# Retention's first weights in other places, five x tiles at the first MLP's end, x stores on ScalarE's queue, one raw ring for the first MLP weights, and token sums by DMA

## The chip, the core and the metric

One core of one Trainium2 chip runs the kernel. Its engines are TensorE (PE in the profile: matmuls and transposes), VectorE (DVE), ScalarE (ACT), GpSimd (POOL) and SyncE (SP, which here only issues DMAs). The metric is the device time of one execution in microseconds; the profile gives the span from the first to the last instruction and busy times within it.

## The reference, cut to what matters

A trunk of two layers over 512 latent tokens and 256 context tokens of width 1024, in float32. Layer 0 is neighbourhood attention beside gated chunks, layer 1 is retention with 8 heads; each is followed by a gated MLP with a convolution over three tokens. Only the latent tokens leave the second layer.

```python
h = modulate(rmsnorm(x, norm_g[i, 0]), sh1, sc1)          # and h_ctx alike
y = hybrid_na_sgu(...) if i % 2 == 0 else retention_mixer(...)
x = x + g1 * rmsnorm(y, norm_g[i, 1])
h = modulate(rmsnorm(x, norm_g[i, 2]), sh2, sc2)
x = x + g2 * rmsnorm(conv_ffn(h, ...), norm_g[i, 3])

def conv_ffn(h, w_in, conv_w, conv_b, w_out):             # D_FF = 2816, two halves
    a = dwconv3(h @ w_in, conv_w, conv_b)
    gate, up = jnp.split(a, 2, axis=-1)
    return (jax.nn.silu(gate) * up) @ w_out

# retention: q, k, v, g = split(h_lat @ w_in); kc, vc from h_ctx; per head a state from
# the context, a scan over chunks of 128 tokens in both directions, a norm, a gate, @ w_out
```

## The kernel before

**Precision.** A float32 matrix is used as a high part (ScalarE's copy, `split`, L68) and a low part (VectorE's difference, L69); a product is three matmuls, high by high, high by low, low by high (`mm3`, L93 to L96).

**Weights.** A block of 128 x 1024 weights (512 KB) is loaded by SyncE into a raw tile (a ring of three, `raw`) and split into a pair of tiles. Pairs `w0` to `w2` belong to a pool that lives through the whole program; further pairs (`w3` and up), and the MLP's extra raw tile `rawu`, belong to the pool of a phase (attention, first MLP, retention, second MLP). A phase's pool is closed before the next opens in the same memory.

**The end of a phase.** `out_last` multiplies the last features by the output weights, token tile by token tile (128 tokens each: 4 and 5 are context, 0 to 3 latent), and for each tile calls `residual` (L317 on): load the old x into `xt`; sums of squares of y on ScalarE (L291), y times the gate on VectorE (L323), a power on GpSimd (L296, L277), x = y * r + x on VectorE (L326), sums of squares again, the store of x to DRAM, then x scaled to unit size (L335, L336). The names of a profile row tell the token: `yb2r` is token tile 2 after attention, `xc3r` tile 3 after the first MLP, `xd` and `yd` after retention. TensorE then transposes the tile (`ht`, `htc`), ScalarE and VectorE modulate it (L364, L366, L412, L414), and the result is split.

**The entry of an MLP.** Columns and weights are taken as 2 x 2 blocks so that from the third block of features on seven block products do the work of eight; the needed sums of token blocks are made once (`block_sums`: `b11`, `b12`, `b21`, `b22` are the staged blocks `sa`, `sb`; L443 to L448), and split into `t1` to `t4` (`hs` holds `t2` and `t4`). The first two features (`plain`) are done without sums: products of `wp00`, `wp10`, `wp01` and `wp11` (gate or up, feature 0 or 1) with the first half of the tokens (`pf`), then with the second (`pf000b` and so on). In the first MLP `wp00`, `wp10` and `wp01` go to `w0`, `w1` and `w2`; in the second `wp00` to `w2`, the others to pairs of the phase's pool (`w5`, `w6`, `w4`).

**The entry of retention.** Head 0 projects k of the context (`rkc`), v of the context (`rn`, 48 matmuls), then k, q, v and the gate g of the latent tokens, half by half (`rk`, `rq`, `rn`). `rwk0`, `rwv00`, `rwv01`, `rwq0`, `rwg00` and `rwg01` are its weights, in `w0` to `w5` in this order.

**What sets the order.** The program is one long list of operations; the framework deals them out to the engines' queues by priority (place in the list) as they become ready in its own estimate, and adds the waits. So SyncE's loads need not stand in the order of the program. Each queue is then worked in order: what stands behind a waiting operation waits too. Layer-0 sums over features go to DRAM by adding DMAs on GpSimd's queue (L1468, L1470). Beside all this, the modulation of later layers (`ada_half`, L214) runs as background work.

Of the kernel before, what the change touches and what calls it, by code (L numbers as in the profile page):

```python
# [8 lines left out]
F32 = mybir.dt.float32  # L9
F32R = mybir.dt.float32r  # L10
# [3 lines left out]
ALU = mybir.AluOpType  # L14
AX = mybir.AxisListType

P = 128
D = 1024
# [22 lines left out]
class Trunk:  # L41
# [273 lines left out]
    def residual(self, t, y, gate, src, last, name, xt):  # L315

        V = self.V  # L317
        self.load(xt, src)
        hv = [slice(0, 512), slice(512, 1024)]
        for n, h in enumerate(hv):  # L320
            self.ssq(y[:, h], f"y{name}{t}", n)
        for h in hv:
            V.tensor_tensor(out=y[:, h], in0=y[:, h], in1=gate[:, h], op=ALU.mult)  # L323
        r = self.rms(f"y{name}{t}")
        for n, h in enumerate(hv):
            V.scalar_tensor_tensor(out=xt[:, h], in0=y[:, h], scalar=r, in1=xt[:, h], op0=ALU.mult, op1=ALU.add)  # L326
            if last:
                self.load(self.out[t * P : (t + 1) * P, h], xt[:, h])
            else:
                self.ssq(xt[:, h], f"x{name}{t}", n)  # L330
        if last:
            return
        self.load(self.xd[t], xt)
        r = self.rms(f"x{name}{t}")
        V.tensor_scalar(out=y[:, hv[0]], in0=xt[:, hv[0]], scalar1=r, scalar2=None, op0=ALU.mult)  # L335
        self.S.activation(y[:, hv[1]], xt[:, hv[1]], AF.Copy, scale=r)  # L336
# [59 lines left out]
    def build_piece(self, l, half, toks, c0, last, xn, ab):  # L396
        S, V = self.S, self.V
        w = P * len(toks)
        s = 1 if toks[0] > 3 else 0
        q = 512 // w  # L400
        for kk in range(KD // q):
            pt = self.ps(f"ht{l}{toks[0]}{kk}", "B", (P, q, w))
            for i in range(q):
                k = q * kk + i
                for j, t in enumerate(toks):
                    self.T.transpose(pt[:, i, j * P : (j + 1) * P], xn[t][:, k * P : (k + 1) * P], self.ident)
            for i in range(q):
                k = q * kk + i
                A, B = ab[:, s, 0, k : k + 1], ab[:, s, 1, k : k + 1]
                h = self.staged(l, half, k, 1)[:, 0, c0 : c0 + w]  # L410
                if i % 2 == 0:
                    S.activation(h, pt[:, i, :], AF.Identity, scale=A, bias=B)  # L412
                else:
                    V.tensor_scalar(out=h, in0=pt[:, i, :], scalar1=A, scalar2=B, op0=ALU.mult, op1=ALU.add)  # L414
        if not last:
            return
        if half:
            n = self.bn
            self.b12 = [
                [self.xp.tile([P, 2, n], F32R, name=f"b12{l}{x}{m}", tag=f"g{x}", bufs=4 if l else 3) for m in range(2)]  # L420
                for x in range(2)
            ]
        for m in range(4):
            src = self.staged(l, half, 2 * m, 2)
            if half and m < 2:
                self.split(self.b12[0][m], self.b12[1][m], src)
            else:
                b = self.blk[(11, 21)[m // 2] if not half else 22]
                ks = slice(2 * (m % 2), 2 * (m % 2) + 2)
                self.split(b[:, 0, ks, :], b[:, 1, ks, :], src)  # L430

    def block_sums(self, l):

        V, n = self.V, self.bn
        put = lambda b, m, src: self.split(b[:, 0, 2 * m : 2 * m + 2, :], b[:, 1, 2 * m : 2 * m + 2, :], src)
        for m in range(2):
            b11, b21 = (self.staged(l, 0, k + 2 * m, 2) for k in (0, 4))
            b12, b22 = (self.staged(l, 1, k + 2 * m, 2) for k in (0, 4))
            if l:
                t1 = self.t2k(f"t1{l}{m}", shape=(P, 2, n))  # L440
            else:
                t1 = self.bp.tile([P, 2, n], F32, name=f"t1{l}{m}", tag=f"y{1 + m}", bufs=1)
            V.tensor_tensor(out=t1, in0=b11, in1=b12, op=ALU.subtract)  # L443
            put(self.blk["t", 1], m, t1)
            V.tensor_tensor(out=b22, in0=b22, in1=b12, op=ALU.subtract)
            put(self.blk["t", 3], m, b22)
            V.scalar_tensor_tensor(out=b22, in0=b22, scalar=-1.0, in1=b11, op0=ALU.mult, op1=ALU.subtract)
            V.scalar_tensor_tensor(out=b12, in0=b22, scalar=-1.0, in1=b21, op0=ALU.mult, op1=ALU.subtract)  # L448
            yield
        hb = self.bp.tile([P, 6144], F32R, name=f"hs{l}", tag="h1", bufs=1)  # L450
        for i, x in enumerate((2, 4)):
            self.blk["t", x] = hb[:, 8 * n * i : 8 * n * (i + 1)].rearrange("p (x k c) -> p x k c", x=2, k=4)
        self.rest = hb[:, 16 * n :]
        for k, x in ((4, 2), (0, 4)):
            for m in range(2):
                put(self.blk["t", x], m, self.staged(l, 1, k + 2 * m, 2))
        yield
# [462 lines left out]
    def retention(self, y, final):  # L920
        S, V, T, G, a = self.S, self.V, self.T, self.G, self.a
        KS = float(np.float32(P) ** np.float32(-0.5))
        with ExitStack() as ctx:
# [10 lines left out]
            self.load(gng, a["gn_col"])  # L934
            w8 = lambda w: [x.rearrange("p (k c) -> p k c", k=4) for x in w]
            qk = lambda h, o, n: self.unit(a["ret_qk"][(o + h) * P : (o + h + 1) * P], f"rw{n}{h}")
            vg = lambda h, o, n: [
                w8(self.unit(a["ret_vg"][(o + h * 2 + i) * P : (o + h * 2 + i + 1) * P], f"rw{n}{h}{i}"))
                for i in range(2)
            ]  # L940
            hd = [{} for _ in range(8)]

            def decay(h):
# [205 lines left out]
            for h in range(8):  # L1149
                vg_tiles(h)  # L1150
                if h == 0:
                    wk = qk(h, 8, "k")
                    self.need(2)
                    k_ctx(h, wk)
                    wv = vg(h, 0, "v")
                    nat(h, wv, 2, "v")
                    self.need(0)
                    wq = qk(h, 0, "q")
                    wg = vg(h, 16, "g")
                    psk = self.ps(f"rk{h}", "A")  # L1160
                    psq = self.ps(f"rq{h}", "A")
# [65 lines left out]
    def ffn(self, l, y, final, gates=None):  # L1227
# [7 lines left out]
        n = self.bn  # L1235
# [5 lines left out]
        with ExitStack() as ctx:  # L1241
            fp = self.phase(ctx, f"ffnp{l}", 0)
            cw = fp.tile([P, 44, 4], F32, name=f"cw{l}", tag="cw")
            self.load(cw, a["conv_col"][:, l * 176 : l * 176 + 176])
            if not first:
                for tag in ("rawu", "wh5", "wl5", "wh6", "wl6", "pre0", "pre1"):
                    fp.tile([P, 1024], F32R if tag[0] == "w" else F32, name=f"at{tag}", tag=tag, bufs=1)
# [35 lines left out]

            def win(j, i):
                r = (l * 44 + (j, NF + j)[i]) * P
                return raw(a["ffn_in"][r : r + P], f"f{l}{i}{j}", i == 1)

            H = [slice(0, 512), slice(512, 1024)]
            halves = lambda u: [[x[:, h] for x in u] for h in H]
# [48 lines left out]
            def weights(j):  # L1338
# [10 lines left out]
                def two():  # L1349
                    u = slot("i", f"wb{j}")  # L1350
                    g, up = st["g"], st["u"]
                    st["s"] = self.t2k(f"s2{j}"), self.t2k(f"s3{j}")
                    V.tensor_tensor(out=st["s"][0], in0=up[:, H[0]], in1=up[:, H[1]], op=ALU.add)
                    V.tensor_tensor(out=st["s"][1], in0=g[:, H[0]], in1=up[:, H[0]], op=ALU.add)
                    d["s", 2], d["s", 3] = halves(u)
                    for x, v in zip((2, 3), st["s"]):
                        self.split(*d["s", x], v)
                    if soon:
                        up_half()

                def three():
                    u = slot("i", f"wc{j}")
                    q3, q4 = self.t2k(f"q3{j}"), self.t2k(f"q4{j}")
                    V.tensor_tensor(out=q3, in0=st["s"][0], in1=st["g"][:, H[0]], op=ALU.add)
                    V.tensor_tensor(out=q4, in0=q3, in1=st["g"][:, H[1]], op=ALU.add)
                    d["q", 3], d["q", 4] = halves(u)
                    for x, v in ((3, q3), (4, q4)):
                        self.split(*d["q", x], v)
# [11 lines left out]
            def plain(js, steps):  # L1380
                d, ps = {}, {}
                for j in js:
                    for i in range(2):
# [22 lines left out]
                            self.split(u[0], u[1], r)  # L1406
                        d[j, i] = halves(u)
                ring["i"] = 0
                self.need(0)
                order = [(j, i) for j in js for i in range(2)]  # L1410
                for x, (j, i) in enumerate(order):
# [73 lines left out]
            for j in range(2, NF):  # L1485
# [7 lines left out]
                product(X, d[11], hb(11), "only")  # L1493
                product(Y, d["s", 2], hb(("t", 1)), "only")
                take(pre, 0, 0, X)
                take(pre, 1, 1, Y, -1.0)
                step()
                if j == 2:
                    nwo = [w_out(0)]
# [2 lines left out]
                    self.bg()  # L1502
                product(X, d["q", 3], hb(("t", 2)), "onto")
                product(Z, d[12], hb(21), "only")
                take(pre, 0, 1, X)
                meet(pre, 0, 0, Z, ALU.add)
                step()
                o(1)
# [11 lines left out]
                if first:  # L1520
                    self.bg()
                product(X, d[22], hb(("t", 4)), "onto")
                take(pre, 1, 0, X, -1.0)
                step()
                o(3)
                gs[j] = conv(j, pre)
# [5 lines left out]
            if first:  # L1532
# [7 lines left out]
                for s in range(2):  # L1540
                    self.load(fin[:, 6 + s], gates[s])
                    gates[s] = fin[:, 6 + s]
                xt = [fin[:, 4], fin[:, 5], fin[:, 8]]
            else:
                fin = fp.tile([P, 4, D], F32, name="fin", tag="blk")
                xt = [fin[:, i] for i in range(4)]
            self.xt = lambda t: xt[t % len(xt)]
            A, B = (
                ([gs[j0 + i] for i in range(GF)], [w_out(j0 + i, r) for i in range(GF)])
                for j0, r in ((LAST, "o"), (LAST + GF, "i"))  # L1550
# [189 lines left out]
```

## Time and profile before

| | |
|---|---|
| timed runs | 1885.12, 1885.89, 1891.13 us (median 1885.89) |
| profiled execution | 1886.89 us, span 1884.7 us |
| TensorE busy | 1801.3 us, 96% |
| VectorE, ScalarE, GpSimd busy | 1404.0, 1028.8, 325.9 us |
| first MLP, retention, second MLP begin at about | 396, 961, 1508 us |

A row of the table of windows says how long each engine was busy in a stretch, with the number of instructions in brackets. A row of the timeline gives start and length of one or more instructions, and in square brackets the idle time before them with what ended it. Two tables of the page name lines of the program with counts and mean times.

### The profile page before, as it was taken

How to read it: one execution, taken by the hardware profiler on the slowest of the kernel's cores; microseconds unless marked ns; L12 is line 12 of the kernel's file. 1: busy time of each engine (PE TensorE's matmuls, PEld its weight loads, DVE VectorE, ACT ScalarE, POOL GpSimd, SP SyncE). 2: the span in 40 equal slices, each digit the busy share in tenths (PEclk: the TensorE clock that was granted, in tenths of full speed). 3: DMA queues.
4: the chain of work that ended last, by engine and by line, in shares of the span. 5: the costliest groups of instructions: out<-in, count | busy, mean ns of one | idle time of the engine just before them, and what ended most of it. 6: DMA issues, size and time to landing. Idle time of an engine off the chain costs nothing. (4 is left out here: it accounts for less than half of the span.)

```text
span 1884.7 us, 28785 instructions
## 1 busy us (share of the span) xinstructions
PE 1801.3 (96%) x10928; PEld 1594.7 (85%) x10928; DVE 1404.0 (74%) x2352; ACT 1028.8 (55%) x1857; POOL 325.9 (17%) x454
## 2 busy tenths in 40 slices
PE   7999999979999999999889999999999989999997
PEld 4887777669989889998779989988999779889996
DVE  4877775689887878777777566676655689988887
ACT  6533555576656465564565435344344477666763
POOL 1103222120122222222121011011001100222221
PEclk9999999989999999999989999999999989999999
DMA  8345321133667768776643323322321225877762
GB/s 289 116 135 151 104 85 40 65 128 101 190 153 152 187 137 177 155 159 142 224 142 113 118 75 100 115 97 68 112 68 53 105 74 151 220 192 190 177 159 95
DMA packets 83375, 250.32 MB, mean 133 GB/s; under 512 B 10898, under 2 KB 11410, under 8 KB 83236
## 3 DMA queue, kind: packets, MB, share of 16 engines
q1 hardware_dynamic: 57348, 199.68, 32.7%
q0 software_dynamic: 25888, 48.80, 15.6%
q8 instruction: 86, 1.41, 0.3%
q14 instruction: 53, 0.43, 0.1%
HBM read 191.81 MB, written 39.85 MB: 123 GB/s over the span
## 5 line engine op out<-in xcount | busy, mean ns | idle before, releaser
L214 DVE SCALAR_TENSOR_TENSOR acc<-ar,cs,acc 128x512 f32<-128x512 f32 x256 | 186.3, 753 | 29.5 <-DMA ar<-in_adaw 19.7
L1470 POOL DMA_DIRECT2D yf<-yp x64 | 55.7, 870 | 261.0 <-ACT yp L1466 238.2
L1321 ACT ACTIVATE cv<-pre,cw 128x770 f32<-128x770 f32 (+1 forms) x88 | 80.9, 923 | 26.9 <-DVE pre L1314 25.5
L1322 DVE SCALAR_TENSOR_TENSOR cv<-pre,cw,cv 128x769 f32<-128x769 f32 (+1 forms) x88 | 77.3, 881 | 6.3 <-ACT cv L1321 6.3
L1309 ACT ACTIVATE pre<-px 128x256 f32<-128x256 f32 (+2 forms) x160 | 54.2, 366 | 44.1 <-PE px L93 36.1
L1325 DVE SCALAR_TENSOR_TENSOR cv<-pre,cw,cv 128x769 f32<-128x769 f32 (+1 forms) x88 | 77.2, 882 | 0.7
L1466 ACT COPY yp<-wf 128x512 f32<-128x512 f32 x118 | 67.8, 577 | 17.7 <-PE wf L96 17.6
L1470 POOL DMA_DIRECT2D yd<-ypg x48 | 42.2, 916 | 133.3 <-ACT ypg L1466 133.0
L1470 POOL DMA_DIRECT2D yd<-yp x48 | 42.7, 904 | 126.2 <-ACT yp L1466 116.9
L1105 POOL TENSOR_SCALAR rrr<-rmv 128x2 f32<-128x2 f32 x16 | 3.1, 192 | 299.3 <-DVE rmv L1102 299.3
L68 ACT ACTIVATE g<-cv 128x770 fp32r<-128x770 f32 (+1 forms) x44 | 32.5, 738 | 31.4 <-DVE cv L1329 31.4
L93 PE MATMUL px<-hs,wd 128*128 128x384 f32 x240 | 45.4, 337 | 0.1
L205 POOL MEMSET acc<- 128x512 f32 x32 | 19.3, 606 | 150.3 <-DVE al L69 131.6
L1314 DVE TENSOR_TENSOR pre<-pre,pz 128x256 f32<-128x256 f32 (+1 forms) x60 | 20.8, 372 | 31.7 <-PE pz L96 31.6
L93 PEld LDWEIGHTS px<-hs,wd 128*128 128x128 f32 x240 | 42.3, 188 | 2.1 <-DVE pre L1314 0.5
L1309 ACT ACTIVATE pre<-py 128x384 f32<-128x384 f32 (+1 forms) x40 | 17.5, 437 | 47.1 <-DVE cv L1325 30.9
L69 DVE TENSOR_TENSOR g<-cv,g 128x770 fp32r<-128x770 f32 (+1 forms) x44 | 36.2, 822 | 7.5 <-ACT g L68 7.3
L1328 ACT ACTIVATE cv<-cv 128x770 f32<-128x770 f32 (+1 forms) x44 | 32.7, 742 | 11.8 <-DVE cv L1325 11.7
L876 ACT ACTIVATE sc<-sc,sst 128x512 f32<-128x512 f32 x32 | 23.1, 721 | 28.4 <-DVE sc L867 28.3
L69 DVE TENSOR_TENSOR rv<-rn,rv 128x512 fp32r<-128x512 f32 x24 | 16.5, 687 | 29.5 <-ACT rv L68 29.5
L1329 DVE TENSOR_TENSOR cv<-cv 128x770 f32<-128x770 f32 (+1 forms) x44 | 36.2, 823 | 2.7 <-ACT cv L1328 1.5
L68 ACT ACTIVATE rv<-rn 128x512 fp32r<-128x512 f32 x24 | 14.3, 595 | 41.9 <-PE rn L96 41.9
(2986 smaller groups left out, 7215.0 us busy)
## 6 DMA issues: line engine op xcount, KB each, us to landing
ar<-in_adaw SPq DMA_DIRECT2D x96, 512.0 KB, 3.7
yf<-yp POOLq DMA_DIRECT2D x64, 256.0 KB, 4.3
yd<-yp POOLq DMA_DIRECT2D x54, 256.0 KB, 5.1
yd<-ypg POOLq DMA_DIRECT2D x54, 256.0 KB, 4.9
fin<-xd SPq DMA_DIRECT2D x10, 512.0 KB
xd<-xd SPq DMA_DIRECT2D x8, 512.0 KB, 2.6
xn<-in_x SPq DMA_DIRECT2D x6, 512.0 KB, 4.9
xb<-in_x SPq DMA_DIRECT2D x6, 512.0 KB, 3.6
```

The costliest lines, as they stand in the source:

```text
L68: self.S.activation(hi, src, AF.Copy)
L69: self.V.tensor_tensor(out=lo, in0=src, in1=hi.bitcast(F32), op=ALU.subtract)
L93: mm = lambda *p, **k: self.nc.tensor.matmul(*p, skip_group_check=True, **k)
L214: V.scalar_tensor_tensor(out=acc[s], in0=raw[:, kk * 512 : kk * 512 + 512], scalar=self.cs[:, 8 * s + k : 8 * s + k + 1], in1=acc[s], op0= ...
L1309: S.activation(pre[:, i, c : c + w], ps[:, b : b + w], AF.Copy, scale=scale)
L1321: S.activation(d, s, AF.Identity, scale=w1, bias=b)
L1322: V.scalar_tensor_tensor(out=d[:, 1:W], in0=s[:, 0 : W - 1], scalar=w0, in1=d[:, 1:W], op0=ALU.mult, op1=ALU.add)
L1325: V.scalar_tensor_tensor(out=d[:, 0 : W - 1], in0=s[:, 1:W], scalar=w2, in1=d[:, 0 : W - 1], op0=ALU.mult, op1=ALU.add)
L1328: S.activation(cv[:, 0], cv[:, 0], AF.Silu)
L1329: V.tensor_tensor(out=cv[:, 0], in0=cv[:, 0], in1=cv[:, 1], op=ALU.mult)
L1466: S.copy(v, ps)
L1470: G.dma_start((yd[t] if first else y[t])[:, o], v, accum_op=ALU.add)
```

## The change

Six edits. The store of x in `residual` is issued by ScalarE instead of SyncE. In `build_piece` and `block_sums` the four token sums are formed with other signs and in another order: in the first MLP four of them are left to adding or copying DMAs on GpSimd's queue (two of them, `b21 += b11`, as soon as the first half is built), in the second MLP all stay on VectorE, two of them moved to `build_piece`; weights' sums and outputs change signs to match. Head 0 of retention puts k into `w2`, v's first half into the tiles `kd0` and `kd1` of its own phase, v's second half into `w0`, q into `w1`. The MLP loads `conv_col` later in the program, and takes the raw tiles of `wp10` and `wp11` from the common ring instead of `rawu`. The first MLP's end has five tiles for x instead of three.

```diff
@@ residual
-        self.load(self.xd[t], xt)
+        self.S.dma_start(self.xd[t], xt)
@@ build_piece, at its end
+        if not half:
+            for m in (0, 2):
+                b11, b21 = (self.staged(l, 0, k + m, 2) for k in (0, 4))
+                if l:
+                    V.tensor_tensor(out=b21, in0=b21, in1=b11, op=ALU.add)
+                else:
+                    self.G.dma_start(b21, b11, accum_op=ALU.add)
@@ block_sums
-        for m in range(2):
-            b11, b21 = (self.staged(l, 0, k + 2 * m, 2) for k in (0, 4))
-            b12, b22 = (self.staged(l, 1, k + 2 * m, 2) for k in (0, 4))
+        st = [[self.staged(l, h, k + 2 * m, 2) for h in (0, 1) for k in (0, 4)] for m in range(2)]
+
+        def add(out, x):
+            if l:
+                V.tensor_tensor(out=out, in0=out, in1=x, op=ALU.add)
+            else:
+                self.G.dma_start(out, x, accum_op=ALU.add)
+
+        for m, (b11, b21, b12, b22) in enumerate(st):
...
-            V.tensor_tensor(out=t1, in0=b11, in1=b12, op=ALU.subtract)
+            V.tensor_tensor(out=t1, in0=b11, in1=b12, op=ALU.add)
+            V.tensor_tensor(out=b22, in0=b22, in1=b12, op=ALU.add)
             put(self.blk["t", 1], m, t1)
-            V.tensor_tensor(out=b22, in0=b22, in1=b12, op=ALU.subtract)
             put(self.blk["t", 3], m, b22)
-            V.scalar_tensor_tensor(out=b22, in0=b22, scalar=-1.0, in1=b11, op0=ALU.mult, op1=ALU.subtract)
-            V.scalar_tensor_tensor(out=b12, in0=b22, scalar=-1.0, in1=b21, op0=ALU.mult, op1=ALU.subtract)
+            if l:
+                V.tensor_tensor(out=b12, in0=b22, in1=b21, op=ALU.add)
+            else:
+                add(b21, b22)
+                self.G.dma_start(b12, b21)
+            add(b22, b11)
+            if l:
+                yield
+        if not l:
             yield
@@ retention, head 0
+                    x = [rp.tile([P, 1024], F32R, name=f"wx{i}", tag=f"kd{i}", bufs=1) for i in range(2)]
+                    self.turn = 2
                     wk = qk(h, 8, "k")
+                    self.turn = 0
+                    wv = [vg1(h, 0, "v", 0, x)]
                     self.need(2)
                     k_ctx(h, wk)
-                    wv = vg(h, 0, "v")
+                    wv.append(vg1(h, 0, "v", 1))
                     nat(h, wv, 2, "v")
                     self.need(0)
                     wq = qk(h, 0, "q")
+                    self.turn = 4
                     wg = vg(h, 16, "g")
...
+            vg1 = lambda h, o, n, i, dst=None: w8(
+                self.unit(a["ret_vg"][(o + h * 2 + i) * P : (o + h * 2 + i + 1) * P], f"rw{n}{h}{i}", dst)
+            )
@@ ffn
-            self.load(cw, a["conv_col"][:, l * 176 : l * 176 + 176])
...
-                return raw(a["ffn_in"][r : r + P], f"f{l}{i}{j}", i == 1)
+                return raw(a["ffn_in"][r : r + P], f"f{l}{i}{j}", i == 1 and j > 1)
...
                 ring["i"] = 0
+                self.load(cw, a["conv_col"][:, l * 176 : l * 176 + 176])
                 self.need(0)
...
                 xt = [fin[:, 4], fin[:, 5], fin[:, 8]]
+                xt.append(fp.tile([P, 1540], F32, name="xtv", tag="cv")[:, :D])
+                xt.append(self.lp.tile([P, D], F32, name="xtg", tag="G1", bufs=1))
...
-            self.xt = lambda t: xt[t % len(xt)]
+            self.xt = lambda t: xt[toks.index(t) % len(xt)]
```

## Rows read from the trace of the kernel before

**Rows 1.** The page: an engine's busy time, share of the span, instructions.
```profile
PE 1801.3 (96%) x10928; PEld 1594.7 (85%) x10928; DVE 1404.0 (74%) x2352; ACT 1028.8 (55%) x1857; POOL 325.9 (17%) x454
```
**Rows 2.** Windows: length; busy (instructions) by engine; granted clock; DMA share; GB/s.
```profile
395.00:400.00 5.00, 0.86 (x2) 0.35 (x2) 4.55 (x7) 4.10 (x9) 2.09 (x3) 0.66 0.06 25
960.00:965.00 5.00, 2.61 (x12) 1.94 (x11) 3.81 (x6) 3.56 (x8) 1.85 (x3) 0.82 0.39 127
1515.00:1520.00 5.00, 0.72 (x4) 0.73 (x5) 3.79 (x8) 3.32 (x8) 1.65 (x2) 0.62 0.27 107
...
425.00:430.00 5.00, 5.00 (x30) 5.00 (x29) 4.67 (x7) 1.29 (x3) 0.00 (x0) 1.00 0.22 83
```
**Rows 3.** Timeline of TensorE at the first MLP's entry: start, length, instruction, idle before.
```profile
401.22 1.54 PE L406 MATMUL ht<-ident,ysg 128*128 128x128 f32 x6 [3.94 <-DVE ysg L335]
...
409.70 1.11 PE L406 MATMUL ht<-ident,ysg 128*128 128x128 f32 x8
412.57 0.44 PE L94 MATMUL pf000b<-b,wp00h 128*128 128x384 f32 x1 [1.76 <-ACT b L68]
...
418.00 0.53 PE L94 MATMUL pf<-hb,wp10h 128*128 128x384 f32 x1
```
**Rows 4.** Timeline of GpSimd, VectorE and ScalarE there.
```profile
395.52 0.94 POOL L296 TENSOR_SCALAR wyb<-ssyb 128x1 f32<-128x1 f32 x1 [5.36 <-ACT jyb L291]
...
401.68 1.22 DVE L69 TENSOR_TENSOR wp00l<-f000r,wp00h 128x1024 fp32r<-128x1024 f32 x1
...
415.06 1.06 ACT L68 ACTIVATE wp10h<-f010r 128x1024 fp32r<-128x1024 f32 x1
```
**Rows 5.** Page and groups by line or tile: counts, mean ns, first and last start.
```profile
L1470 POOL DMA_DIRECT2D yd<-yp x48 | 42.7, 904 | 126.2 <-ACT yp L1466 116.9
...
yd<-yp POOLq DMA_DIRECT2D x54, 256.0 KB, 5.1
...
L447 DVE SCALAR_TENSOR_TENSOR sb<-sb,sa 128x768 f32<-128x768 f32 x2 | 1.9, 953 | 0.0
...
L93 PE MATMUL px<-hs,wc2h x8: 336/337/442, 455.1 to 457.0; 128*128 128x384 f32 x8
...
L69 DVE TENSOR_TENSOR hs<-sb,hs x4: 951/954/957, 431.9 to 442.5; 128x768 fp32r<-128x768 f32 x4
```
**Rows 6.** Timeline of ScalarE, TensorE and SyncE at retention's entry.
```profile
935.20 1.05 ACT L68 ACTIVATE rwv01h<-rwv01r 128x1024 fp32r<-128x1024 f32 x1
...
961.10 0.39 PE L94 MATMUL rkc<-h0c,rwk0h 128*128 128x256 f32 x1 [0.46 <-ACT rwk0h L68]
...
963.54 0.58 PE L96 MATMUL rkc<-h0c,rwk0l 128*128 128x256 f32 x1 [1.94 <-DVE rwk0l L69]
...
965.42 1.66 PE L358 MATMUL htc<-ident,fin 128*128 128x128 f32 x8
...
968.52 0.28 PE L94 MATMUL rn<-rwv00h,h0c 128*128 128x256 f32 x1
...
974.02 0.28 PE L96 MATMUL rn<-rwv01h,h1c 128*128 128x256 f32 x1
...
974.52 0.33 SPq L54 DMA_DIRECT2D xd<-fin  x1
...
978.83 0.38 ACT L971 ACTIVATE kc<-rkc 128x256 f32<-128x256 f32 x1 [1.73 <-DMA xd<-fin]
...
980.75 0.55 PE L94 MATMUL rq<-h0c,rwq0h 128*128 128x256 f32 x1 [2.84 <-DMA dist<-in_dist]
```
**Rows 7.** Timeline of GpSimd, TensorE and ScalarE at the second MLP's entry.
```profile
1490.22 0.30 POOL L296 TENSOR_SCALAR wyd<-ssyd 128x1 f32<-128x1 f32 x1 [8.20 <-ACT jyd L291]
...
1512.19 1.51 POOL L296 TENSOR_SCALAR wyd<-ssyd 128x1 f32<-128x1 f32 x1 [4.89 <-ACT jyd L291]
...
1519.28 1.97 PE L406 MATMUL ht<-ident,yr 128*128 128x128 f32 x8 [5.92 <-DVE sb L414]
1519.38 1.04 ACT L68 ACTIVATE wp01h<-f101r 128x1024 fp32r<-128x1024 f32 x1
...
1523.38 1.06 ACT L68 ACTIVATE wp10h<-f110r 128x1024 fp32r<-128x1024 f32 x1
```

More of the change, by code (lines that the diff above doesn't have):

```diff
@@ L936, in retention @@
             qk = lambda h, o, n: self.unit(a["ret_qk"][(o + h) * P : (o + h + 1) * P], f"rw{n}{h}")
[L937 to L940, printed above, removed]
+            vg1 = lambda h, o, n, i, dst=None: w8(
+                self.unit(a["ret_vg"][(o + h * 2 + i) * P : (o + h * 2 + i + 1) * P], f"rw{n}{h}{i}", dst)
+            )
+            vg = lambda h, o, n: [vg1(h, o, n, i) for i in range(2)]
             hd = [{} for _ in range(8)]
@@ L1352, in two @@
                     st["s"] = self.t2k(f"s2{j}"), self.t2k(f"s3{j}")
-                    V.tensor_tensor(out=st["s"][0], in0=up[:, H[0]], in1=up[:, H[1]], op=ALU.add)
-                    V.tensor_tensor(out=st["s"][1], in0=g[:, H[0]], in1=up[:, H[0]], op=ALU.add)
+                    V.tensor_tensor(out=st["s"][0], in0=up[:, H[0]], in1=up[:, H[1]], op=ALU.subtract)
+                    V.tensor_tensor(out=st["s"][1], in0=g[:, H[0]], in1=up[:, H[0]], op=ALU.subtract)
                     d["s", 2], d["s", 3] = halves(u)
@@ L1363, in three @@
                     q3, q4 = self.t2k(f"q3{j}"), self.t2k(f"q4{j}")
-                    V.tensor_tensor(out=q3, in0=st["s"][0], in1=st["g"][:, H[0]], op=ALU.add)
+                    V.tensor_tensor(out=q3, in0=st["s"][0], in1=st["g"][:, H[0]], op=ALU.subtract)
                     V.tensor_tensor(out=q4, in0=q3, in1=st["g"][:, H[1]], op=ALU.add)
@@ L1495, in ffn @@
                 take(pre, 0, 0, X)
-                take(pre, 1, 1, Y, -1.0)
+                take(pre, 1, 1, Y)
                 step()
@@ L1504, in ffn @@
                 product(Z, d[12], hb(21), "only")
-                take(pre, 0, 1, X)
+                take(pre, 0, 1, X, -1.0)
                 meet(pre, 0, 0, Z, ALU.add)
@@ L1522, in ffn @@
                 product(X, d[22], hb(("t", 4)), "onto")
-                take(pre, 1, 0, X, -1.0)
+                take(pre, 1, 0, X)
                 step()
```

## The prediction

> **What bounds the kernel now.** I read the page's first lines, then the table of 5 us windows, then the waits and the timeline of the windows where TensorE dips. TensorE is busy 1801.3 of 1884.7 us [rows 1]: inside the MLP loops and the retention heads it runs at its own pace (29 or 30 matmuls of 384 columns in 5 us, 0.17 us each, in the last row of [rows 2]), so work taken from another engine there is worth nothing. What can be won lies where TensorE dips, and three dips lie at what the change touches: the entry into the first MLP (0.86 us busy of the 5 from 395), into retention (2.61 of 5 from 960) and into the second MLP (0.72 of 5 from 1515) [rows 2]. After each dip matmuls go at half the rate for a while; the granted clock in these windows is 0.66, 0.82 and 0.62, a mix of its two levels, 1.2 and 2.4 GHz.
>
> At the entries the same thing is seen: the first touch of any tile of the new phase comes just behind the last store of x. Retention's `kc` comes at 978.83, 4.3 us after the store issued at 974.52, though TensorE had gone from its matmuls to the next at 968.52 [rows 6]; in the second MLP `wp01h`, whose weights are asked for before the last token's transposes, starts only beside them, at 1519.38 [rows 7]. So a new phase's pool is handed out whole, when all of the old one is done; the tiles `w0` to `w2`, which live in a pool of the whole program, are handed on one by one.
>
> My sum is against the profiled execution, 1886.9 us (span 1884.7 and 2.2 around it), which is 1.0 above the median 1885.89 of the three timed runs.
>
> **The change, part by part.**
>
> *First MLP, common ring.* Before, weight `f010r` was loaded into `rawu`, a tile of the new phase, so its split `wp10h` came at 415.06 [rows 4] and its products at 418.00 [rows 3]. In the common ring it can be loaded long before, and its place `w1` is free with the last output matmul, as `wp00h`'s was. TensorE then has 24 more products ready at 409.7. Between there and 418.00 it had 8.3 us; 1.1 are transposes, and the 14 products from 412.57 on are worth 14 x 0.17 = 2.4 at full rate. Lost: 8.3 - 1.1 - 2.4 = 4.8, and 7 products more run at half rate from 418.00 on (0.53 us each there), 7 x 0.15 = 1.0. So 5.8 at most. Against it, VectorE has to do one more weight split (1.22, as `wp00l` [rows 4]) ahead of the half-1 tokens; that half is what the 24 products cover, so at least I charge 1.2. At worst nothing is gained, since the transposes still wait for tokens 2 and 3.
>
> *First MLP, token sums by DMA.* Four VectorE operations of 0.95 go (two `b22` and two `b12` sums [rows 5]), 3.8 us. TensorE does not wait for them: the first use of `hs` is at 455.1, and its last split at 442.5 [rows 5]. Eight GpSimd DMAs come in. One issue takes 0.90 on GpSimd, one transfer of 256 KB 5.1 to land [rows 5]; at 384 KB an estimate by size alone is 7.7 at most, and three in a row 23, against 12.6 of slack plus the 11 in which the old splits ran, so they stay hidden, just. But two of the eight can go as soon as the first half's splits end, about when `wyb` of token 2 comes: on the queue on which it stands at 395.52 [rows 4], and TensorE's next transposes wait for that token [rows 3]. That is 0 to 1.8; I take half, 0.9, because `wp00l` (401.68) is wanted for the same products and is as late.
> Net of the first MLP: 5.8 - 1.2 - 0.9 = 3.7 gained; ends: 3.0 lost (1.2 + 1.8, nothing gained) and 5.8.
>
> On GpSimd there is a rule that speaks against this. The rows: the step `wyd` took 0.30 on GpSimd at 1490.22 and 1.51 at 1512.19, with two VectorE operations beside it [rows 7]. Hindered in the same way, two issues cost 2 x 1.2 = 2.4 more. The Trainium skill (SBUF — State Buffer, "A bandwidth-pool intuition that's wrong (but worth ruling out)" and the box before it) says that a POOL-queue DMA needs GpSimd to write descriptors and that some VectorE copies shut GpSimd out for their whole length; there a DMA of 0.62 us took 3.1. The row at 1512.19 agrees in kind; no run here shows such a DMA held. By the row the result is a rival below.
>
> *Retention's first weights.* Before: k in `w0`, v in `w1` and `w2`, q in the new phase. After: k in `w2`, v's first half in the new phase (`kd`), its second in `w0`, q in `w1`. `w2` is free early: `rwv01h` filled it at 935.20, while TensorE still waited for k's split into `w0` at 961.10 and 963.54 [rows 6]. So k's waits of 0.46 and 1.94 go, and with them the half rate behind: about 12 of `rkc`'s 24 matmuls at 0.21 in place of 0.115, 1.2, and the 8 transposes at 965.42 (1.66 in place of 1.03), 0.6. Together 4.2 us, by which the build of token columns 0 to 255 is earlier, and token 3's chain, which stood behind it on ScalarE and VectorE, may be too; with it the last store and the hand-over at 978.83. In return v is late: the 48 matmuls from 968.52 to 974.02 (5.5 us) were done before the hand-over and no longer can be; q's 24 (24 x 0.115 = 2.8) can. So 2.7 less work is covered. Net 4.2 - 2.7 = 1.5 gained. Ends: v's matmuls stand in TensorE's order ahead of k's and q's, 5.5 + 2.8 = 8.3 lost; the wait of 2.84 at 980.75 goes as well and 13 matmuls after it run at full rate (1.3), 4.2 + 2.8 + 1.3 = 8.3 gained.
>
> *Second MLP.* `f110r` is loaded early, but its place `w5` belongs to the new phase, so the 5.92 us wait at 1519.28 [rows 7] stays. `wp10h` moves from 1523.38 to about 1519.4; products then fill the time to 1523.38 in part: 1.7 gained (15 of 256 columns at 0.115). VectorE's two added sums of 0.69 come in ahead of token 3's chain, which the wait at 1519.28 is for: 1.2 lost. In the ring `f110r`, `f101r` and `f111r` push out `f102r`, so one split (2.3 over two engines) moves from the idle gap to behind it; VectorE was idle through most of that gap and is no longer so behind it, which I leave in the ends. Net 0.5 gained, between 2.5 lost (both costs, no gain) and 3.
>
> *Stores on ScalarE's queue.* Sixteen. SyncE's issue took 0.33 each and no ScalarE issue is in the trace; I take the same. Each stands behind the sum of squares of the same half, which waited for the same VectorE result, and ahead of a wait for GpSimd of 0.4 to 1.5, so 0; all of them in the open would be 16 x 0.33 = 5.3. SyncE's loads no longer queue behind stores, but the loads that mattered waited for places. *Five x tiles, later `cw` load, turned signs:* no wait of TensorE in [rows 3] or [rows 6] is for an x load or for `cw`; 0, bounded by one issue-to-landing of the kind in [rows 6], 4.3, either way.
>
> Sum: 3.7 + 1.5 + 0.5 = 5.7 off, 1886.9 - 5.7 = 1881.2, and 1880 as a median of timed runs (1.0 lower).
>
> **The rivals.** A time within 5.7 us (0.3%) of before is no change: that is about what a measurement of this kernel can tell.
> 1. *Retention's v waits for the hand-over (slower).* If TensorE's order has v's 48 matmuls before k's and q's, all stop until `kd` is handed out near 978.8: 8.3 lost there, 3.0 lost in the first MLP if its transposes still gate: 1886.9 + 8.3 + 3.0 - 0.5, less 1.0, 1897; with the first MLP's gain, 1890. For it: everything of that phase waited for the store. Against: the order is made by readiness. It decides once the hand-over is later than about 971, when k's and q's work runs out. Price 4 to 11, middle 1893.
> 2. *Nothing moves.* At each entry the token chain and not the weights ends the wait (3.94 at 401.22, 5.92 at 1519.28): 1884 to 1887.
> 3. *Hand-over earlier too.* Retention's upper end, 8.3, with 5.8 of the first MLP: 1886.9 - 14.1 - 0.5 - 1.0 = 1871. For it: ScalarE and VectorE each lose a split from token 3's chain; against: v's and q's splits take their place.
> 4. *GpSimd shut out by VectorE:* 2.4 more on token 2's chain: 1882.5.
>
> **How the numbers follow.** Forecast 0.40 (0.22 of it below 1880.2, 0.18 above), rival 3 0.20, rival 2 0.18, rival 4 0.05, rival 1 0.17 (0.16 of it over 1891.6). Faster 0.22 + 0.20 = 0.42; same 0.18 + 0.18 + 0.05 + 0.01 = 0.42; slower 0.16. The forecast alone spans 1876 to 1884; taking in most of rivals 2 and 3 and the near end of rival 1, the range is 1870 to 1890.
>
> **What would show it.** Right: products of `wp10` before those of `pf000b`, no gap between 409.7 and 418; `rkc` straight behind the last output matmul, and the x store's landing 3 to 5 us earlier against that matmul. Wrong: `rn` matmuls waiting for `rwv00h` ahead of `rk`; GpSimd's DMA issues ahead of `wyb` with TensorE's transposes later; a MLP loop that no longer runs at 0.17 a matmul.

## The result: slower by 0.37%

The changed kernel takes 1895.71 us (median of 20 runs, 1888.15 to 1900.92), the kernel before 1888.26 in the same comparison (20 runs, 1882.39 to 1897.78): a ratio of 1.0037, 95% interval 1.0023 to 1.0051, some 7 us more. Forecast were 1880 and a range of 1870 to 1890. The profiled execution took 1894.45 us, its span is 1892.6, 7.9 above the span before.

First I laid the two traces beside each other by landmarks on TensorE, each the first or last start of a tile's matmuls, and for the hand-over the issue of `dist`, the first load into retention's pool:

| landmark, us | before | after | lead |
|---|---|---|---|
| last output matmul of attention (`watc`) | 393.3 | 389.3 | 4.0 |
| first `px` of the first MLP | 446.3 | 436.9 | 9.4 |
| last `px` of the first MLP | 916.2 | 914.6 | 1.6 |
| its last output matmul (`wf0C`) | 959.8 | 952.8 | 7.0 |
| hand-over (`dist`) | 978.7 | 978.1 | 0.6 |
| first `wrA`, retention's last output group | 1478.9 | 1485.8 | -6.9 |
| first `px` of the second MLP | 1544.8 | 1550.0 | -5.2 |
| last output matmul | 1873.4 | 1880.7 | -7.3 |

So the entry into the first MLP did gain, 5.4 us beyond the lead that was there already: `wp10` is split early there and its products run at once, ScalarE's and then TensorE's row of after (against 415.06 and 418.00 in [rows 4] and [rows 3]):

```profile
397.08 1.05 ACT L68 ACTIVATE wp10h<-f010r 128x1024 fp32r<-128x1024 f32 x1
398.18 0.69 PE L94 MATMUL pf<-hb,wp10h 128*128 128x384 f32 x1
```

Then 7.8 are lost in its loop, 5.4 are won at its output, 6.4 are lost again before the hand-over, and 7.5 go behind it. The page's first line of after, against [rows 1]:

```profile
PE 1798.3 (95%) x10928; PEld 1593.9 (84%) x10928; DVE 1402.0 (74%) x2350; ACT 1028.0 (54%) x1857; POOL 327.1 (17%) x462
```

The windows of after, those of [rows 2] and one of 20 us (columns as there), and that longer one of before:

```profile
395.00:400.00 5.00, 2.77 (x8) 2.21 (x9) 4.15 (x6) 4.08 (x8) 3.55 (x4) 0.51 0.57 106
960.00:965.00 5.00, 0.00 (x0) 0.00 (x0) 3.13 (x5) 1.39 (x4) 2.47 (x4) 0.67 0.70 245
1515.00:1520.00 5.00, 3.62 (x18) 3.22 (x17) 3.40 (x7) 4.13 (x8) 0.76 (x2) 0.50 0.25 101
425.00:430.00 5.00, 5.00 (x30) 5.00 (x29) 4.69 (x6) 4.87 (x8) 1.91 (x3) 1.00 0.56 144
960.00:980.00 20.00, 4.69 (x17) 3.31 (x18) 12.09 (x21) 11.05 (x25) 5.21 (x8) 0.54 0.33 116
```
```profile
960.00:980.00 20.00, 15.51 (x115) 14.45 (x113) 12.54 (x20) 12.59 (x27) 5.88 (x7) 0.91 0.32 108
```

The pace inside the loop is as before (30 matmuls in 5 us). The large difference is retention's entry: of 20 us TensorE works 4.69 in place of 15.51, and the granted clock of the stretch is 0.54 in place of 0.91. The timeline of TensorE there shows why; in brackets is the idle time before an instruction and what ended it (it answers to [rows 6]):

```profile
953.24 0.39 PE L96 MATMUL wf0C<-fo021h,g 128*128 128x512 f32 x1
953.47 0.28 PE L94 MATMUL rkc<-h0c,rwk0h 128*128 128x256 f32 x1
...
956.23 0.28 PE L96 MATMUL rkc<-h0c,rwk0l 128*128 128x256 f32 x1
958.30 0.88 PE L358 MATMUL htc<-ident,fin 128*128 128x128 f32 x6 [1.79 <-DVE fin L335]
967.29 1.97 PE L358 MATMUL htc<-ident,fin 128*128 128x128 f32 x8 [8.12 <-DVE hc L366]
...
977.56 1.54 PE L358 MATMUL htc<-ident,yf 128*128 128x128 f32 x6 [6.59 <-DVE yf L335]
...
981.19 0.55 PE L94 MATMUL rn<-wx,h0c 128*128 128x256 f32 x1
981.54 0.41 PE L94 MATMUL rk<-h0c,rwk0h 128*128 128x256 f32 x1
...
991.75 0.28 PE L94 MATMUL rq<-h0c,rwq0h 128*128 128x256 f32 x1
```

and ScalarE and SyncE, the two timelines of the same stretch:

```profile
952.97 1.07 ACT L68 ACTIVATE rwv01h<-rwv01r 128x1024 fp32r<-128x1024 f32 x1 [0.17 <-PE wf0C L96]
953.94 1.04 ACT L68 ACTIVATE rwq0h<-rwq0r 128x1024 fp32r<-128x1024 f32 x1
...
975.23 0.33 ACTq L333 DMA_DIRECT2D xd<-fin  x1
979.61 1.05 ACT L68 ACTIVATE wx<-rwv00r 128x1024 fp32r<-128x1024 f32 x1
978.09 0.33 SPq L54 DMA_DIRECT2D dist<-in_dist  x1
```

`rkc` runs straight behind the output matmuls (953.24, 953.47), as hoped. Then none of retention's products is in TensorE's order until `rn` on `wx`, v's first half; `wx` is split at 979.61, behind the hand-over at 978.09. The second half of v and q, split on ScalarE by 955, stand in TensorE's order behind it, and k's products of the latent tokens too: `rn` 48 and `rk` 24 matmuls that ran before the hand-over now run after it, 72 x 0.115 = 8.3 us. TensorE's waits carry the names of the token chain only because that is what it has left to do.

### The profile page after: what moved, and what is told of

Its sections match the earlier page's. It is cut to its first block, busy times and chain, and to the rows that moved or that the text cites. A ratio compares the mean times of both kernels' runs of the same rounds, so it can differ in the third digit from the quotient of the medians.

```text
span 1892.6 us, 28784 instructions
## 1 busy us (share of the span) xinstructions
PE 1798.3 (95%) x10928; PEld 1593.9 (84%) x10928; DVE 1402.0 (74%) x2350; ACT 1028.0 (54%) x1857; POOL 327.1 (17%) x462
## 5 line engine op out<-in xcount | busy, mean ns | idle before, releaser
L214 DVE SCALAR_TENSOR_TENSOR acc<-ar,cs,acc 128x512 f32<-128x512 f32 x256 | 185.6, 751 | 28.1 <-DMA ar<-in_adaw 16.7
L1491 ACT COPY yp<-wf 128x512 f32<-128x512 f32 x118 | 67.9, 577 | 16.7 <-PE wf L96 16.5
L1333 ACT ACTIVATE pre<-py 128x384 f32<-128x384 f32 (+1 forms) x40 | 17.5, 437 | 44.9 <-DVE cv L1349 23.5
```

What stands on the lines that cost most here:

```text
L214: V.scalar_tensor_tensor(out=acc[s], in0=raw[:, kk * 512 : kk * 512 + 512], scalar=self.cs[:, 8 * s + k : 8 * s + k + 1], in1=acc[s], op0= ...
L1333: S.activation(pre[:, i, c : c + w], ps[:, b : b + w], AF.Copy, scale=scale)
L1491: S.copy(v, ps)
```

## The experiments

Each was timed beside the kernel before on the same chip; a difference in us is (ratio - 1) x the median of before there (1885.7 for 1 to 4, 1885.5 for 5 to 8, 1883.9 for 9 to 12). Kernels 4 and 6 have 6 runs each, the others 12. The changed kernel stands at +7.0 (4.3 to 9.6) in this measure. Landmarks come from one profiled execution each, which lay up to 7.4 us from the kernel's median (8 and 9). The first MLP's loop, from the first to the last `px`, took 463.4 to 469.9 us in four kernels whose MLP is the same (before, 2, 7 and 8), so a stretch counts here only where it repeats.

**1. The change without its retention weights, and 2. these alone.**

```
-                    x = [rp.tile(..., name=f"wx{i}", tag=f"kd{i}", bufs=1) for i in range(2)]
-                    self.turn = 2
                     wk = qk(h, 8, "k")
-                    self.turn = 0
-                    wv = [vg1(h, 0, "v", 0, x)]
...
-                    wv.append(vg1(h, 0, "v", 1))
+                    wv = vg(h, 0, "v")
                     nat(h, wv, 2, "v")
...
-                    self.turn = 4
```

> The changed kernel with Retention's first weights put back where they were (k in w0, v in w1 and w2, q in the new phase); all else as changed. Theory A: the loss is v's first half in a tile of the new phase, for which TensorE stood idle 15.3 us between 960 and 980 (4.5 before). Then rn's matmuls come back ahead of the last x store, the idle time from 960 to 980 falls to 4 to 7 us, and the time is 6 to 10 us below the changed kernel, 1886 to 1890. Rival B: the loss is in the chain of token steps on ScalarE, VectorE and GpSimd (the stores on ScalarE's queue stretch it): then the time stays within 3 us of the changed kernel, 1893 to 1898.

> The kernel before with nothing changed but Retention's first weights (k in w2, v's first half in kd of the new phase, its second in w0, q in w1). Theory A: rn's 48 matmuls wait for the hand-over behind the last x store, some 8 us lost: 1894 to 1898. Rival B: no loss without the other parts, 1885 to 1890.

Measured: without, 1890.53, ratio 1.0024 (1.0010 to 1.0039), +4.5 us; alone, 1891.09, 1.0025 (1.0011 to 1.0040), +4.7. The times fall between the theories: the edit by itself is a loss, smaller than 8, and undoing it doesn't bring the kernel back to before (the difference of 2.5 to the changed kernel is within the intervals). The traces are clearer. In 1 TensorE's idle time from 960 to 980 falls to 5.3 us, as theory A had it. From the hand-over to the first `wrA` it is 507.4 to 508.3 us in all four kernels with v in `kd` (the changed one, 2, 3 and 4 below) and 500.2 without (before, 1): 7.2 to 8.1 lost, near the 8.3 of the prediction's lower end. All ten kernels without v in `kd` have 497.2 to 502.7, so the least that the traces leave is 4.7. Alone the edit also makes the hand-over earlier: 60.5 us behind the last `px` against 62.5. So the net is 6 in the trace, and theory A holds for the place. That undoing it isn't enough says that other parts lose too.

**3. The change with the token sums on VectorE, and 4. with the stores on SyncE** (one line of each).

```
-            self.G.dma_start(out, x, accum_op=ALU.add)   # first MLP
+            V.tensor_tensor(out=out, in0=out, in1=x, op=ALU.add)
```
```
-        self.S.dma_start(self.xd[t], xt)
+        self.load(self.xd[t], xt)
```

> The changed kernel with the first MLP's token sums back on VectorE (signs as changed). In the changed kernel ScalarE and VectorE stood 3.8 and 3.5 us behind the last sum's DMA, and TensorE 4.05 us at 447.4 for fo00h. Theory A: that wait goes, but the first MLP's lead is lost at its end anyway, where the token chain and not TensorE sets the hand-over, so the time is 0 to 3 us below the changed kernel. Rival C: the DMA sums are a loss of their own that reaches the end, 4 us or more below the changed kernel. If VectorE sets the loop's pace, the lead at the end of the loop is no larger than the 1.6 us of the changed kernel.

> The changed kernel with the x stores back on SyncE's queue. Theory A: within 2 us of the changed kernel, the hand-over within 1.5 us of 978.1. Rival B: the stores on ScalarE's queue stretch the token chain, so the hand-over comes 3 us or more earlier and the time is 4 to 8 us lower.

Measured: 3, 1888.90, 1.0027 (1.0010 to 1.0043), +5.1; 4, 1895.13, 1.0056 (1.0035 to 1.0076), +10.6. For 3 that is 1.9 below the changed kernel, in theory A's range, but within the intervals. Its trace speaks against theory A's reason: the first MLP's loop takes 468.2 us against 477.7, and it is 4.7 ahead of the changed kernel at the last `px` and still 4.8 at the hand-over, 8.2 at the last output matmul; but this profiled execution was 3.3 below its kernel's median, and the times don't show it. For 4 neither is shown: no faster than the changed kernel. In its trace the six tokens' chain at the first MLP's end is shorter, 41.8 us from the first token's last step to the last one's against 44.6, and the hand-over 2.2 earlier, but that did not show in the time. What follows from 1, 3 and 4 is only that no single part undone brings the kernel back to before.

**5. What is left without retention's weights, DMA sums and ScalarE stores** (the ring, `cw`, x tiles and signs, with what these change in the second MLP).

> The changed kernel without its retention weights, its DMA sums and its stores on ScalarE: what is left of the change is the common raw ring, the later cw load, the five x tiles and the turned signs. Theory A (retention's weights cost 7 to 8 us behind the hand-over, stores on ScalarE 2.7 in the token chain, DMA sums 4 to 6 in the first MLP, the ring gains 2 to 4 at its entry): 1 to 5 us below before, 1881 to 1885; from the hand-over to the first matmul of retention's output 500 us as before. Rival D (the ring itself costs what it gains, VectorE being busy there): within 2 us of before.

Measured: 1879.51, 0.9971 (0.9955 to 0.9986), -5.5 us (-8.5 to -2.6): just past theory A's 1 to 5, and outside rival D's 2. The entry from attention's end to the first `px` is 46.8 us against 53.0 before. Behind the hand-over it is 497.5, not theory A's 500.

**6. The token sums by DMA alone** (on the kernel before, with their signs; the core of it). With two more sums ahead of these and both halves of the features it is eight DMAs, six sums and two copies. Two things come with them as in the changed kernel: the sums of both halves are given out as one piece (one `yield` for two, which 3 takes back too), and in the second MLP the sums stay on VectorE in their new places. What these are worth by themselves was not run.

```
-            V.scalar_tensor_tensor(out=b22, in0=b22, scalar=-1.0, in1=b11, op0=ALU.mult, op1=ALU.subtract)
-            V.scalar_tensor_tensor(out=b12, in0=b22, scalar=-1.0, in1=b21, op0=ALU.mult, op1=ALU.subtract)
+            self.G.dma_start(b21, b22, accum_op=ALU.add)
+            self.G.dma_start(b12, b21)
+            self.G.dma_start(b22, b11, accum_op=ALU.add)
```

> The kernel before with nothing but the first MLP's token sums as GpSimd DMAs, and the signs that go with them. Theory A: the last sum's DMA lands after ScalarE and VectorE have come to it in their order, so the first MLP's loop is 3 to 7 us longer than before: 1888 to 1893. Rival E: without the ring the plain products begin later and the sums have the slack that the prediction gave them: 1884 to 1887.

Measured: 1898.33, 1.0062 (1.0038 to 1.0086), +11.7 us: worse than either view, the dearest part of the change. From first to last `px` the four kernels with all eight DMA sums took 476.5 to 478.0 us, all the others 463.4 to 470.9, in the mean 477.3 against 467.9. The changed kernel's trace shows how; first GpSimd, then ScalarE, VectorE and TensorE in its timelines:

```profile
423.38 0.92 POOL L449 DMA_DIRECT2D sa<-sb  x1 [12.07 <-DVE sb L457]
428.09 0.57 POOL L464 DMA_DIRECT2D sb<-sa  x1 [3.79 <-ACT cv L1345]
428.65 0.91 POOL L449 DMA_DIRECT2D sb<-sa  x1
429.21 1.23 POOL L449 DMA_DIRECT2D sa<-sb  x1
435.33 0.57 POOL L464 DMA_DIRECT2D sb<-sa  x1 [4.89 <-DMA sa<-sb]
435.89 0.89 POOL L449 DMA_DIRECT2D sb<-sa  x1
```
```profile
440.12 0.85 ACT L68 ACTIVATE hs<-sb 128x768 fp32r<-128x768 f32 x1 [3.84 <-DMA sb<-sa]
...
446.33 1.04 ACT L68 ACTIVATE fo00h<-fo00r 128x1024 fp32r<-128x1024 f32 x1
441.00 0.96 DVE L69 TENSOR_TENSOR hs<-sb,hs 128x768 fp32r<-128x768 f32 x1 [3.54 <-ACT hs L68]
447.42 1.22 PE L94 MATMUL wf<-fo00h,g 128*128 128x512 f32 x2 [4.05 <-ACT fo00h L68]
```

Each copy (L464) waits on GpSimd's in-order queue for the sum ahead of it to land, 4.7 us (423.38 to 428.09) and 6.1 (429.21 to 435.33); the second half's sums stand behind the first copy, and the last sum lands at 440.0. (The bracket at 428.09 names ScalarE, but the sum of 423.38 landed at 427.5, and in 6 the same bracket names it.) ScalarE and VectorE stand 3.84 and 3.54 at `hs`, and with them everything behind it in their order; TensorE pays with 4.05 at `fo00h`. In kernel 6 it is starker, these windows of it first, the same of before below:

```profile
435.00:445.00 10.00, 10.00 (x59) 10.00 (x58) 2.92 (x3) 4.01 (x6) 1.45 (x2) 1.00 0.49 133
455.00:465.00 10.00, 6.10 (x24) 5.15 (x23) 10.00 (x14) 6.93 (x11) 0.00 (x0) 0.83 0.34 105
```
```profile
435.00:445.00 10.00, 10.00 (x59) 10.00 (x59) 8.51 (x11) 9.75 (x16) 0.00 (x0) 1.00 0.18 54
455.00:465.00 10.00, 9.87 (x54) 9.40 (x55) 9.32 (x16) 5.36 (x11) 0.68 (x1) 1.00 0.20 66
```

VectorE works 2.92 of 10 us while the DMAs run, where it had 8.51 before, and is busy throughout later, when TensorE works only 6.10 of 10; TensorE's two waits there are for ScalarE, 2.01 for `fo00h` and 1.89 for `pre`.

**7. The stores on ScalarE's queue alone** (experiment 4's edit the other way round, on the kernel before).

> The kernel before with nothing but the x stores on ScalarE's queue. Theory A: the chain of the six tokens at the first MLP's end, 41.8 to 42.4 us from the first token's last step to the last one's with stores on SyncE, becomes 44.5 to 45.1, and the output matmuls end some 5 us earlier without use: 1 to 3 us above before, 1887 to 1889. Rival F: the earlier output matmuls are worth something: 1 to 4 us below before.

Measured: 1891.09, 1.0035 (1.0020 to 1.0049), +6.6 us, twice theory A's upper end; the direction is right, the place only in part. The output matmuls from last `px` to last `wf0C` take 38.1 to 38.2 us with such stores (changed, 1, 3 and 7) and 42.9 to 43.9 in all the others, 5 us won; and the chain of tokens takes 44.5 to 46.0 against 41.6 to 42.7. ScalarE's timeline in 7, then in before:

```profile
930.47 0.33 ACTq L333 DMA_DIRECT2D xd<-fin  x1
930.95 0.19 ACT L291 ACTIVATION_READ_ACCUMULATOR jxc<-fin 128x1 f32 x1
932.22 0.72 ACT L336 ACTIVATE fin<-fin,xc4r 128x512 f32<-128x512 f32 x1 [1.08 <-POOL xc4r L277]
932.85 0.61 ACT L291 ACTIVATE jyc<-fin 128x512 bf16<-128x512 f32 x1
```
```profile
932.70 0.19 ACT L291 ACTIVATION_READ_ACCUMULATOR jxc<-fin 128x1 f32 x1
932.79 0.61 ACT L291 ACTIVATE jyc<-fin 128x512 bf16<-128x512 f32 x1
933.31 0.19 ACT L291 ACTIVATION_READ_ACCUMULATOR jyc<-fin 128x1 f32 x1
933.96 0.72 ACT L336 ACTIVATE fin<-fin,xc4r 128x512 f32<-128x512 f32 x1 [0.46 <-POOL xc4r L277]
```

The issue itself costs nothing (0.33 on the queue beside a running instruction). But the next token's first sum of squares `jyc`, 0.61 + 0.19, which before filled the wait for GpSimd's `xc4r`, now stands behind it: from the first to the second token's last step 7.5 us in 7 and 6.9 before, and so on for each token. TensorE's 5 us go unused, since the hand-over waits for the chain: it comes 65.0 us behind the last `px` against 62.5. The same stands behind attention, where theory A did not look: the six tokens' chain there takes 39.8 to 41.5 us with such stores (changed, 1, 3, 7 and 11) and 36.6 to 38.4 in all the others, and the first `px` comes 2.0 later in 7 than before. Where the rest of the 6.6 lies was not found.

**8. Retention's k in `w2`, v in `w0` and `w1`, q in the new phase** (on the kernel before).

```
+                    self.turn = 2
                     wk = qk(h, 8, "k")
                     self.need(2)
                     k_ctx(h, wk)
+                    self.turn = 0
                     wv = vg(h, 0, "v")
                     nat(h, wv, 2, "v")
                     self.need(0)
+                    self.turn = 3
                     wq = qk(h, 0, "q")
```

> The kernel before with k of Retention's first head in w2, v in w0 and w1, q in the new phase as before: k's place is free sooner and no v waits for the hand-over. Theory A: k's waits of 0.5 and 1.9 us go, but the token chain sets the hand-over and 500 us follow it as before: within 2 us of before, 1884 to 1888. The prediction's own view: 4 us less, 1881 to 1882.

Measured: 1882.16, 0.9980 (0.9965 to 0.9996), -3.8 us (-6.6 to -0.8). That is nearer to the prediction's view than to theory A, though the interval reaches into theory A's 2. What repeats in the traces is the hand-over: with stores on SyncE at the first MLP's end it comes 60.3 to 60.6 us behind the last `px` in the six kernels with k in `w2` (2, 4, 8, 9, 11 and 12) and 61.4 to 63.5 in the four with k in `w0` (before, 5, 6 and 10). In 8 TensorE has `rn` in the trace from 957.4 on, ahead of the hand-over at 971.10, and its granted clock from 945 to 985 is 1.00 (0.90 before, 0.71 in the changed kernel):

```profile
945.00:985.00 40.00, 34.43 (x251) 31.38 (x250) 31.37 (x47) 27.19 (x56) 11.25 (x14) 1.00 0.41 136
```

From the hand-over to `wrA` it is 497.5 us, 2.7 less than before; 5, with the old places, has the same 497.5, so that this part comes from k's place isn't shown.

**9 to 12. Combinations.** 9 is 5 with 8's retention weights. 10 is 5 without the two added x tiles. 11 is 9 with ScalarE stores behind attention and retention only, 12 is 9 with two of the eight sums by DMA:

```
# 11
+        (self.nc.sync if name == "c" else self.S).dma_start(self.xd[t], xt)
# 12, first MLP, as soon as the first half's splits are made
+                    self.G.dma_start(b21, b11, accum_op=ALU.add)
```

> The ring, cw, x tiles and signs of the changed kernel (as in the run e5_ring_xtiles), and k of Retention's first head in w2, v in w0 and w1, q in the new phase. Theory A: the two gains, 5.5 and 3.8 us against before, lie at different places and add: 7 to 11 us below before, 1874 to 1879. Rival: the hand-over is set by the token chain in both, so the second adds nothing: 1879 to 1881.

> As e5_ring_xtiles, without the five x tiles (three as before). The prediction put the x tiles at 0: then within 2 us of e5_ring_xtiles, 1878 to 1882, with the chain of the six tokens at the first MLP's end at 41.8 to 42.6 us. Rival: the x loads are what makes the chain shorter: 3 us or more above it.

> As e9_ring_k_w2, with the x stores on ScalarE's queue behind attention and behind retention, and on SyncE's behind the first MLP. Theory A: the loss of stores on ScalarE lies in the token chain at the first MLP's end; at the other two places they win 0 to 3 us together (the stretch from retention's output to the second MLP's loop was 64.2 to 64.8 us with them and 65.2 to 66.3 without): 0 to 3 us below e9_ring_k_w2. Rival: they lose wherever a token chain is the bound: 2 to 5 us above it.

> As e9_ring_k_w2, with the first two of the eight token sums (second half of the features plus the first, ready with the first half of the tokens) as GpSimd DMAs and the others on VectorE. Theory A: the DMAs lose because hs waits for the last of three in a row; these two are not last in a row, so within 2 us of e9_ring_k_w2, and TensorE shows no wait for fo00h over 1 us. Rival: GpSimd's issue itself, ahead of the token steps, is the loss: 3 us or more above it.

Measured: 9, 1876.07, 0.9954 (0.9935 to 0.9972), -8.7 us; 10, 1880.83, 0.9980 (0.9965 to 0.9996), -3.8; 11, 1877.61, 0.9970 (0.9954 to 0.9986), -5.7; 12, 1878.37, 0.9971 (0.9953 to 0.9988), -5.5. 9 beats both kernels: 0.9954 against 1 and against the changed kernel's 1.0037. That is about the sum of the gains of 5 and 8, but the intervals of 5 and 9 overlap, so that they add isn't shown. The x tiles (5 against 10) are worth 1.7 us by the ratios, within the intervals. 11 and 12 lie 3 us above 9, where their rivals had them and not theory A, but less than can be told apart. 11 keeps ScalarE's stores behind attention, where 7 shows the longer chain: its entry to the first `px` is 49.7 us against 46.8 in 9. In 12's trace TensorE has no wait for `fo00h` (4.05 to 4.59 in the changed kernel, 1 and 4): the two sums that nothing is queued behind don't bring back what was seen in 6. The page's first line of 9:

```profile
PE 1790.9 (96%) x10928; PEld 1584.1 (85%) x10928; DVE 1405.1 (75%) x2356; ACT 1026.9 (55%) x1857; POOL 325.9 (17%) x454
```

## Why the prediction was wrong

- *First MLP, common ring: right, and at the entry worth more than forecast.* The products of `wp10` come ahead of those of `pf000b` (its split is at 397.08, 415.06 in [rows 4]) and the gap of [rows 3] is closed. Against the 5.8 at most, 10's entry, from attention's end to the first `px`, is 6.1 shorter (46.9 against 53.0); the 1.2 that I charged against it was not seen there. Of that 3.8 (0.8 to 6.6) reached the end, with the second MLP's edits in it.
- *Token sums by DMA, "so they stay hidden, just": this step failed first.* I set three DMAs in a row against the slack of `hs`'s first use by TensorE. The slack that mattered is ScalarE's and VectorE's, which take `hs` in order, ahead of the weights that TensorE needs next. Before, `hs` was split from 431.9 to 442.5 between other work [rows 5]; after, from 440.1 on and in one piece. The DMAs were even quicker than I allowed: 6.7 or less to land, not 7.7, and 16.7 from the first issue of the row at 423.38 to the last landing, not 23. Predicted 0.9 lost (for GpSimd's queue, 0 to 1.8), measured 11.7 in 6.
- *Retention's first weights: this step failed too.* Rival 1 is what happened at this place, its condition included: "It decides once the hand-over is later than about 971"; it was at 978.1. Against its 8.3 the traces show 7.2 to 8.1 behind the hand-over, and alone the edit costs 4.7 (2.1 to 7.5). That the whole time of 1895.71 lies in rival 1's range of 1890 to 1897 is luck: two other edits lose too, and one gains. I forecast a gain of 1.5 since "q's 24 can" run ahead of it: q did not, at 991.75 it is the last of the four. I also took k's 4.2 us to reach the last store. About 2 did where the stores stayed on SyncE (experiment 8). The store goes by the chain of token steps on ScalarE, VectorE and GpSimd, which begins 17.8 us behind the last `px` in all fourteen traces: the output matmuls' lead of 7.0 became 0.6 at the hand-over. The x store's landing was forecast 3 to 5 us earlier against the last output matmul; the hand-over behind it is 6.4 later against that (25.3 against 18.9).
- *Stores on ScalarE's queue at 0: failed.* The issues cost nothing that the rows show, as said; the order on ScalarE that came with them did, 6.6 us alone. My worst case counted issues and no reordering.
- *Second MLP: near enough.* TensorE still waits for the transposes, 9.6 us in all between 1480 and 1560 against 8.7; the stretch from the first `wrA` to the first `px` is 64.2 us against 65.9, 1.7 gained where I had 0.5. How much of it is this edit's isn't shown: with stores on SyncE the stretch is 65.1 to 65.9 in five kernels with the change's second MLP (4, 5, 9, 10 and 12) and 65.9 to 66.3 in three without (before, 2 and 8), and 7, with ScalarE's stores and without it, took 67.2. The end "2.5 lost (both costs, no gain)" does not follow from the costs named beside it: 1.2 and the split's 2.3 would be up to 3.5.
- *GpSimd shut out (rival 4): not seen.* The two issues ahead of `wyb` took 1.90 together and delayed it (the rows below; the sum of squares that it waits for had ended at 396.2). That is the 0 to 1.8 for which I charged 0.9. But the rule of the Trainium skill named there (SBUF — State Buffer, "A bandwidth-pool intuition that's wrong (but worth ruling out)"), a POOL-queue DMA held for a whole VectorE operation, shows in no issue here: those of the sums took 0.57 to 1.23. Why the sums' landings spread from 4.0 to 6.7 stays open.

```profile
395.84 1.90 POOL L437 DMA_DIRECT2D sa<-sa  x2 [5.22 <-DVE hb L69]
397.82 1.09 POOL L296 TENSOR_SCALAR wyb<-ssyb 128x1 f32<-128x1 f32 x1
```

That the DMA sums, ScalarE's stores and retention's weights each lose, and the rest gains, is shown by the runs. What stays open: the four parts alone come to -5.5 + 11.7 + 6.6 + 4.7 = 17.5 us, all together to 7.0. They share their place (the hand-over takes only the later of two chains, so that losses may hide behind each other), but how the 10 us fall out between them was not measured.

## What to carry to other kernels

A lead of the busiest engine is worth only what the next hand-over lets through: find the chain that sets the hand-over (here the last tokens' steps on the small engines) before counting what TensorE gains ahead of it. When work is put into a buffer that becomes free later, count everything behind its first user in the in-order queue, not that user alone. When an operation is moved off an engine, look at who waits in order for its result: the engine that was relieved may stand idle for it.

## What was not expected of the hardware

The sums' accumulating DMAs of 384 KB within the core's memory landed 4.0 to 6.7 us after their issue in the changed kernel, its two copies of the same size after 2.6. The 256 KB that GpSimd's queue adds into DRAM took 5.1 [rows 5]. What cost time was landings in a row: three of them, with the issues and waits between, make up the 16.7 us from 423.38 on. The Trainium skill (DMA: Bandwidth & Descriptors, "Anatomy of one DMA — SWDGE (gpsimd) path") states a fixed cost of about 2.0 us and a small part by size, by which an estimate is 2.9; the copies agree with it (2.6), the accumulating ones took longer. The mean granted clock of the runs goes with the time: 0.980 over the 20 runs of the changed kernel, 0.984 over those of before beside the experiments, 0.987 in 9. A stall of TensorE is paid twice, by the idle time and by matmuls at the lower of the two levels behind it: in the changed kernel the twenty that follow 981.19 are 0.21 us apart, later ones 0.12.
